# Hybrid delta-rule and attention block: four VectorE/GpSimd assignments and the slot of the v transposes

## The chip, the core and the metric

The kernel runs on one core of a Trainium2 chip. A core has five instruction queues that run side by side and meet through semaphores: TensorE (PE, matrix products and transposes, with its weight loads listed as PEld), VectorE (DVE), ScalarE (ACT), GpSimd (POOL) and SyncE (SP, which here issues nearly all DMAs). Each queue runs its instructions in the order in which they were written into it. The metric is the device time of one execution in microseconds; the time before is 1368.79 us, the median of 3 runs (1368.75 to 1371.78).

## The reference, cut to what matters

One layer of a diffusion backbone works on 512 latent tokens and 256 context tokens of width 2048. Both groups of heads read one input projection.

```
h  = rms_norm(x)*(1+scale)+shift          # adaLN; the same for the context hc
qkv_g, z_g, gates, q_a, k_a, v_a, z_a = split(h @ w_in)      # and hc @ w_in
# group A, 8 heads of 128: conv of 5 taps, silu, then per 64-token chunk
a     = strict_lower((k*beta) k^T * decay);  t_inv = (I + a)^-1
v_new = u - w S;  o = (q e^g) S + intra v_new;  S = S e^{g_last} + (k e^{..})^T v_new
o_gdn = o_forward + flip(o_backward)       # two scans, starting from the context's state
gdn   = rms_norm(o_gdn) * silu(z_g)
# group B, 8 query heads on 2 key heads: rms-normed q, k, rotary positions on latents, softmax
attn  = softmax(q k^T) v * silu(z_a)
y     = concat(gdn, attn) @ w_out;   out = rms_norm(x + gate*y)
```

## The kernel before, in words

Products are made from passes on fp32r operands: each 128x512 piece of a weight is loaded (`wraw`), cast on ScalarE to a high part (`whi`, L129), and the low part is the difference of the two (`wlo`, L130). The helper `split` takes the engine of that subtraction as an argument and uses GpSimd where none is given. Three buffers each hold `wraw`, `whi` and `wlo`. Every output needs three matmuls per 128 rows: high by high, high by low activations, low by high.

The kernel has these stages. Up to about 150 us it normalises the input, forms the modulation and projects the first tiles. From about 150 us to 930 us it runs the 8 heads' delta-rule scans one after the other; this is the stage that the change touches. From about 930 us to 1180 us it runs the attention, with the z projections as filler (their `wlo` is on GpSimd too, through `z_piece`). The last stage is the output projection, whose `wlo` (`wlo_wo`) is on VectorE already.

In the scan stage TensorE's order is written out by hand (`manual_schedule` for PE): a scan of one head is a generator with 12 steps, and each step hands TensorE three groups of work with a pause (a slot) between them, 35 slots in all. In a pause, `pull(n)` takes as many columns of matmuls from `feeding()`: the projections of the k, q and v of later heads, of the attention's k, v, q and of some z, all through `proj_steps` (L152 to L180), which fetches one weight piece per 12 or 24 matmuls. A step of the scan has this chain: two matmuls on the state (`ks`, L852, L854), the right side `r` on VectorE (L866, two halves), a matmul with the inverse (`ts`, L875), its scaling on ScalarE (`vs`, `vn`, L879, L882), the update matmuls (L886) and the new state `st` on VectorE (L892). The old state times its decay (`sd`) is formed on GpSimd meanwhile (L240 through `mul`). The pulls of F1, F2 and F3 columns (3900, 2700, 3200) are what TensorE has to do while it waits for `r`, for `vs` and for `st`.

The order on VectorE, ScalarE, GpSimd and SyncE in this stage is set by a planner that simulates the program: an engine takes the ready instruction of the highest priority. Priority follows program order, and blocks marked `first_of_all()` (the scan's own steps) or `soon()` are moved ahead.

Beside the scan of head h, `gdn_prep(h+1)` prepares the next head in steps at the slots `PREP_AT`. The steps before the v transposes make `ktok`, the sums of squares, the gate differences `gr` (L681: a row of cumulated gates minus a column, then L684 and an exponential), the matrix `AT` in place of `gr`, and the inverse of its 16x16 blocks, a chain of 28 small VectorE operations on `NE` (L738, L740). Then two steps transpose v on TensorE and scale it into `vtok` on ScalarE (L751, L753); the second of them also issues four loads of `DD` on SyncE (L758) and one transpose on VectorE (L763). The last four steps finish the inverse into `UU`, whose last parts VectorE copies (L821). At the end of a scan the two directions are added (L902, L903). Beside the scan of the last head runs `attn_prep()`: it norms k and q and calls `rope_apply` three times (L944, through `mul` at L240), which multiplies by the sine table (`rt2`), multiplies in place by the cosine table, and adds.

Of the kernel before, what the change touches and what calls it, by code (L numbers as in the profile page):

```python
# [11 lines left out]
ALU = mybir.AluOpType  # L12
# [56 lines left out]
def build(tc, a):  # L69
    nc = tc.nc  # L70
    V, S, G, T, SY = nc.vector, nc.scalar, nc.gpsimd, nc.tensor, nc.sync
# [31 lines left out]
    def hpass(k, hi, lo):  # L103

        return (hi, [t[:, k] for t in hh]), (hi, [hl(m, k) for m in range(2)]), (lo, [t[:, k] for t in hh])
# [13 lines left out]
    gsc = {}  # L119
# [6 lines left out]
    def split(raw, nm, lo_eng=None):  # L126
        hi = wp.tile([128, 512], F32R, tag="whi", bufs=3, name=f"whi_{nm}")
        lo = wp.tile([128, 512], F32R, tag="wlo", bufs=3, name=f"wlo_{nm}")
        S.copy(hi, raw)  # L129
        (lo_eng or G).tensor_tensor(out=lo, in0=raw, in1=hi, op=ALU.subtract)  # L130
        return hi, lo

    def wpiece(src, nm, shape, lo_eng=None):
        raw = wp.tile([128, 512], F32, tag="wraw", bufs=3, name=f"wraw_{nm}")
        v = raw
        if shape is not None:
            v = raw.rearrange("p (a b) -> p a b", b=shape)
        SY.dma_start(v, src)
        hi, lo = split(raw, nm, lo_eng)
        if shape is not None:  # L140
            hi = hi.rearrange("p (a b) -> p a b", b=shape)
            lo = lo.rearrange("p (a b) -> p a b", b=shape)
        return hi, lo
# [6 lines left out]
    def proj_tile(col, nm, pl, pc=None):  # L150
        for _ in proj_steps(col, nm, pl, pc):
            pass  # L152

    def proj_steps(col, nm, pl, pc=None):


        for kq in range(4):
            src = w_in[kq * 512:(kq + 1) * 512, col:col + 128].rearrange("(k p) c -> p k c", p=128)
            hi, lo = wpiece(src, f"{nm}_{kq}", 128)
            passes = [(kq * 4 + k4, n, lw, rt) for k4 in range(4)  # L160
                      for n, (lw, rt) in enumerate(hpass(kq * 4 + k4, hi[:, k4], lo[:, k4]))]

            def one(out, m, k, n, lw, rt):
                T.matmul(out, lhsT=lw, rhs=rt[m], start=k == 0 and n == 0, stop=k == KT - 1 and n == 2,  # L164
                         skip_group_check=True)

            if pc is not None and kq == 0:
                for out, m, n_ in ((pl, 0, SEQ), (pc, 1, CTX)):
                    for x in passes:
                        one(out, m, *x)  # L170
                        yield n_
                continue
            for x in passes:
                one(pl, 0, *x)
                if pc is not None:
                    one(pc, 1, *x)
                yield SEQ if pc is None else SEQ + CTX
# [11 lines left out]
    def btile(shape, nm):  # L189
        return PB.tile(shape, F32, tag="b", name=nm)  # L190
# [4 lines left out]
    def take(pl, pc, raw=None, eng=None):  # L195

        raw = next_craw() if raw is None else raw
        copy = S.copy if eng is None else eng.tensor_copy
        if pc is not None:
            copy(raw[:, 2:2 + CTX], pc)  # L200
        copy(raw[:, CTX + 4:CTX + 4 + SEQ], pl)
        return raw
# [33 lines left out]
    def silu(eng, out, x, t):  # L236
        eng.scalar_tensor_tensor(out=out, in0=t, scalar=1.0, in1=x, op0=ALU.add, op1=ALU.mult)

    def mul(eng, out, x, y):
        eng.tensor_tensor(out=out, in0=x, in1=y, op=ALU.mult)  # L240
# [347 lines left out]
    def kq_of(h):  # L588
        if h not in kqs:
            kqs[h] = qkp.tile([128, 8, 128], F32, tag="kq", bufs=3, name=f"kq{h}")  # L590
        return kqs[h]

    def gdn_post_k(h, raw):
        kq = kq_of(h)
        kc = kcs[h] = qkp.tile([128, 2, 2, 64], F32, tag="kc", bufs=2, name=f"kc{h}")
        acc, e, off = conv(8 + h, f"k{h}", raw, True)
        x, y = [t[:, off:off + SEQ].rearrange("p (c t) -> p c t", t=64) for t in (acc, e)]
        silu(V, kq[:, 0:4, 0:64], x[:, 0:4], y[:, 0:4])
        silu(V, kq[:, 4:8, 64:128], x[:, 4:8], y[:, 4:8])
        x, y = [t[:, 0:CTX].rearrange("p (c t) -> p c t", t=64) for t in (acc, e)]  # L600
        silu(V, kc[:, :, 0], x[:, 0:2], y[:, 0:2])
        silu(V, kc[:, :, 1], x[:, 2:4][:, ::-1], y[:, 2:4][:, ::-1])
# [18 lines left out]
    def gdn_prep(h):  # L621


        nm = f"h{h}"
        kq, kc, vv = kqs[h], kcs[h], vvs[h]
        UU, IB = UUs[h % 2], IBs[h % 2]
        col = slice(h * 12, h * 12 + 12)
        gr = gp.tile([128, 12, 64], F32, tag="gr", bufs=1, name=f"gr{nm}")
        for s in range(2):
            src = growd[s:s + 1, col].rearrange("s r t -> s (r t)").to_broadcast([64, 768])  # L630
# [7 lines left out]
        t2 = btile([128, 4, 128], f"t2{nm}")  # L638
# [17 lines left out]
        for p in range(2):  # L656
# [18 lines left out]
                        in0=gsc["beta"][:, col].rearrange("p (v q) -> p v q", v=2),  # L675
                        in1=rk2.unsqueeze(1).to_broadcast([128, 2, 6]), op=ALU.mult)
# [1 line left out]
        mul(V, cc[:, 2], cc[:, 0], gsc["esuf"][:, col])  # L678


        G.tensor_tensor(out=gr, in0=gr, in1=gsc["gcum"][:, col].unsqueeze(2).to_broadcast([128, 12, 64]),  # L681
                        op=ALU.subtract)
        for v in range(2):
            V.tensor_tensor(out=gr[:, v * 6:v * 6 + 6], in0=gr[:, v * 6:v * 6 + 6],  # L684
                            in1=masks[v].unsqueeze(1).to_broadcast([128, 6, 64]), op=ALU.min)
# [36 lines left out]
        for half in range(2):  # L722
            for blk in range(2):
                b, bi = half * 64 + blk * 32, half * 2 + blk
                cb = slice(blk * 32, blk * 32 + 32)
                for v in range(2):
                    src = AT[b:b + 32, v * 6:v * 6 + 6, cb] if v == half else NT[b:b + 32, :, cb]
# [6 lines left out]
        with tc.high_priority(offset=1500):  # L734
            for m in range(14, 0, -1):
                n = 15 - m
                tv = tm[:, :m * n].rearrange("w (j i) -> w j i", i=n)
                V.tensor_tensor(out=tv, in0=NE[:, 0:m, m:m + 1].to_broadcast([96, m, n]),  # L738
                                in1=NE[:, m:m + 1, m + 1:].to_broadcast([96, m, n]), op=ALU.mult)
# [44 lines left out]
        for bi in range(4):  # L784
            half, b = bi // 2, bi * 32
            for v in range(2):
                src = (DD if v == half else DT)[b:b + 32, v * 6:v * 6 + 6]
# [36 lines left out]
    def gdn_scan(h):  # L824

        nm = f"h{h}"
        kq, kc = kqs[h], kcs[h]
# [4 lines left out]
        oq = gp2.tile([128, 2, 4, 128], F32, tag="oq", bufs=1, name=f"oq{nm}")  # L832
        osb = oq[:, 0]
        kss = stile([128, 2, 256], f"ks{nm}", "k")
        steps = [(0, 0), (0, 1), (1, 1), (1, 0)] + [(0, p) for p in range(2, 6)] + [(1, p) for p in range(5, 1, -1)]
        for si, (v, p) in enumerate(steps):
# [8 lines left out]
            if si == 0:  # L845
                r = vtok[:, p]
            else:
                ks = kss[:, si % 2].rearrange("q (d e) -> q d e", d=2)
                r = gp2.tile([128, 128], F32, tag="r", bufs=1, name=f"r{nm}_{si}")
# [9 lines left out]
                with first_of_all():  # L859
# [5 lines left out]
                    for rows, d in halves:  # L865
                        V.scalar_tensor_tensor(out=r[rows], in0=ks[rows, d], scalar=gsc["negeg"][rows, gcol:gcol + 1],  # L866
                                               in1=vtok[rows, p], op0=ALU.mult, op1=ALU.add)
# [31 lines left out]
        ms = gp2.tile([128, 4], F32, tag="ms", bufs=2, name=f"ms{nm}")  # L899
        oc = gp2.tile([128, 8, 64], F32, tag="oc", bufs=1, name=f"oc{nm}")  # L900
        jk = oc[:, 0:2].rearrange("p c t -> p (c t)")
        G.tensor_tensor(out=oq[:, 1], in0=osb, in1=oq[:, 1], op=ALU.add)  # L902
        V.tensor_tensor(out=osb, in0=oq[:, 1], in1=o, op=ALU.add)  # L903
        for p in range(4):
            S.activation(jk, osb[:, p], AF.Square, accum_out=ms[:, p:p + 1])
# [15 lines left out]
    def swapped(x):  # L921

        return x.rearrange("p t (a s r) -> p (t a) s r", a=2, s=2)[:, :, ::-1]
# [17 lines left out]

    def rope_apply(y, tb, t2):

        mul(G, t2.rearrange("p t (a s r) -> p (t a) s r", a=2, s=2), swapped(y),  # L944
            tb[:, 1].rearrange("p t (a s r) -> p (t a) s r", a=2, s=2))
        mul(V, y, y, tb[:, 0])
        V.tensor_tensor(out=y, in0=y, in1=t2, op=ALU.add)
# [76 lines left out]
        split_from(tp.rearrange("p t c -> p (t c)"), *A["qt"])  # L1024

    F1, F2, F3 = 3900, 2700, 3200
    PREP_AT = (0, 2, 4, 6, 8, 10, 12, 27, 29, 31, 33)

    def soon():
        return tc.high_priority(offset=1500)  # L1030
# [4 lines left out]
    with tc.high_priority(offset=4000):  # L1035
        raws = [take(klat, cctx[:, 0]), take(qlat, None), take(vlat, cctx[:, 1], None, V),
                take(klat1, cctx1[:, 0], xraw[0]), take(qlat1, None, xraw[1])]
# [24 lines left out]
    def feed_q(h):  # L1062
        pl = PP.tile([128, SEQ], F32, tag="pl", name=f"ql{h}")
        yield from proj_steps(COL_Q + h * 128, f"q{h}", pl)
        gdn_post_q(h, take(pl, None))
# [54 lines left out]
    def pull(n):  # L1120
        debt[0] += n
        while debt[0] > 0:
            c = next(feed, None)
            if c is None:
                debt[0] = 0
                return
            debt[0] -= c

    def run(gen, *pulls):

        for n in pulls:
            pull(n)
            if next(gen, gen) is gen:
                return
        for _ in gen:
            pull(2000)

    g0, g1 = gates(0, 1), gates(1, NH)
# [7 lines left out]
    with first_of_all():  # L1146
        next(g0, None)
    prep = gdn_prep(0)
    for i, n in enumerate((3000, 5500, 5500, 4000, 14000, 6000)):
        pull(n)  # L1150
        next(prep, None)
        if i == 4:
            gdn_post_k(1, raws[3])
    pull(3000)
    next(g1)
    pull(9000)
    with first_of_all():
        next(g1)
    gdn_post_q(1, raws[4])
    es_x.close()  # L1160
    run(g1, 14000)
    es1.close()
    gp2 = es_g.enter_context(tc.tile_pool(name="gp2", bufs=1, reuse_waits="tile"))
    UUs.append(gp2.tile([128, 12, 128], F32, name="UU1"))
# [3 lines left out]
    for h in range(NH):  # L1168
# [3 lines left out]
        if h + 1 < NH:  # L1172
            prep, prep_at = gdn_prep(h + 1), PREP_AT
        else:
# [4 lines left out]
            prep, prep_at = attn_prep(), range(1, 36, 2)  # L1179
# [334 lines left out]
    for c in range(4):  # L1514
# [3 lines left out]
        if c < 3:  # L1518
            ops = [PO.tile([128, 512], F32, tag="po", name=f"po{c}_{t}") for t in range(4)]
            for k in range(KT):  # L1520
                hi, lo = wpiece(w_out[k * 128:(k + 1) * 128, cs_], f"wo{c}_{k}", None, V)
# [6 lines left out]
        for k in range(KT):  # L1528
            hi = op_.tile([128, 512], F32R, name=f"wlh{k}")
            lo = op_.tile([128, 512], F32R, name=f"wll{k}")  # L1530
# [5 lines left out]
        for t in range(4):  # L1536
# [5 lines left out]
            f = fr[:, t:t + 1]  # L1542
# [36 lines left out]
```

## Time and profile before

| what | us |
|---|---|
| median of 3 runs (lowest, highest) | 1368.79 (1368.75, 1371.78) |
| the profiled execution | 1373.23 |
| its span, first to last instruction | 1371.5 |
| GpSimd busy in the span | 458.2 |
| VectorE busy in the span | 781.6 |
| TensorE busy in the span | 1271.3 |

The profiled execution lies 4.4 us above the median, and 1.7 us of it lie outside the span. Busy time of an engine is the time in which at least one of its instructions ran. In the list of waits a row names the engine, what the waiting instruction makes and its line, what it waited for, and then the sum of the waits in us, their number and the longest. In a timeline a row has the start, the duration, the engine, the line, the operation, output and inputs, and in brackets the idle time of the engine just before and what ended it. PEclk is the clock granted to TensorE as a share of full speed.

### The profile page before, as it was taken

To read this page: it belongs to the slowest core of one execution; us is meant where nothing else is said; L and a number is where in the kernel's file an instruction comes from. 1 tells how busy PE (TensorE), PEld (TensorE's weight loads), DVE (VectorE), ACT (ScalarE), POOL (GpSimd) and SP (SyncE) were. 2 spreads that over 40 slices of the span, in tenths; PEclk is the share of its full clock that TensorE was granted. 3 is DMA by queue.
4 is the path that set the end of the run, shared out by engine and by line. 5 is a ranking of instruction groups with operands and counts; after the bars stand their busy time and mean duration, and the time that the engine had idled before them with its cause. 6 is when DMAs were issued, how large, how long until landed. Compare 5 with 4: busy or idle time off the path is not lost. (4 is left out here: it accounts for less than half of the span.)

```text
span 1371.5 us, 24428 instructions
## 1 busy us (share of the span) xinstructions
PE 1271.3 (93%) x9226; PEld 1032.2 (75%) x9226; DVE 781.6 (57%) x1662; ACT 583.7 (43%) x1464; POOL 458.2 (33%) x437
## 2 busy tenths in 40 slices
PE   6899998999899999999899998998999999999997
PEld 4566777877788778877787777777888788777785
DVE  5455594766846666485664524316788877544322
ACT  4222542535345454544545434434455444433211
POOL 1323232434344253434334344443233232020330
PEclk9999999999999999999999999999999999999998
DMA  9999233221332223231222443347344343564212
GB/s 342 323 334 348 56 94 85 60 63 44 71 75 70 50 66 65 71 72 53 51 59 70 98 128 100 89 135 226 108 124 146 100 130 109 189 225 146 92 39 92
DMA packets 227001, 164.54 MB, mean 120 GB/s; under 512 B 62210, under 2 KB 198491, under 8 KB 225859
## 3 DMA queue, kind: packets, MB, share of 16 engines
q1 hardware_dynamic: 226586, 162.87, 40.9%
q8 instruction: 73, 1.20, 0.4%
q14 instruction: 45, 0.37, 0.1%
q10 hardware_dynamic: 297, 0.11, 0.0%
HBM read 148.85 MB, written 14.08 MB: 119 GB/s over the span
## 5 line engine op out<-in xcount | busy, mean ns | idle before, releaser
L130 POOL TENSOR_TENSOR wlo_z<-wraw_z,whi_z 128x512 fp32r<-128x512 f32 x44 | 67.3, 1544 | 141.0 <-ACT whi_z L129 128.3
L240 POOL TENSOR_TENSOR sdh<-sth,egl 128x256 f32<-128x256 f32 x80 | 55.1, 689 | 144.4 <-DVE sth L892 99.7
L866 DVE SCALAR_TENSOR_TENSOR rh<-ksh,negeg,vtokh 64x128 f32<-64x128 f32 x176 | 61.3, 348 | 55.3 <-PE ksh L854 45.5
L871 ACT ACTIVATE oqh<-ksh,egsw 64x128 f32<-64x128 f32 x128 | 46.4, 362 | 103.7 <-DVE rh L866 95.8
L147 PE MATMUL po<-wlo_wo,mh 128*128 128x512 f32 x192 | 77.7, 405 | 3.7 <-DVE wlo_wo L130 3.7
L892 DVE TENSOR_TENSOR sth<-sdh,tsh 128x256 f32<-128x256 f32 x80 | 33.6, 419 | 80.3 <-PE tsh L886 73.1
L148 PE MATMUL po<-whi_wo,ml 128*128 128x512 f32 x192 | 77.6, 404 | 0.0
L146 PE MATMUL po<-whi_wo,mh 128*128 128x512 f32 x192 | 76.9, 403 | 0.5 <-ACT whi_wo L129 0.5
L130 DVE TENSOR_TENSOR wlo_wo<-wraw_wo,whi_wo 128x512 fp32r<-128x512 f32 x48 | 37.7, 793 | 63.8 <-ACT whi_wo L129 63.8
L1360 PE MATMUL zl<-hhL,whi_z 128*128 128x512 f32 x176 | 74.0, 421 | 0.0
L1360 PE MATMUL zl<-hhL,wlo_z 128*128 128x512 f32 x176 | 69.7, 396 | 0.1
L1360 PE MATMUL zl<-hL,whi_z 128*128 128x512 f32 x176 | 69.6, 396 | 0.0
L886 PE MATMUL tsh<-vsh,ktok 128*128 128x128 f32 x352 | 58.2, 289 | 8.7 <-ACT vsh L879 5.6
L886 PEld LDWEIGHTS tsh<-vsh,ktok 128*128 128x128 f32 x352 | 49.1, 197 | 18.8 <-ACT vsh L879 8.7
L1401 DVE SCALAR_TENSOR_TENSOR gacc<-graw,scol,gacc 128x512 f32<-128x512 f32 x60 | 60.0, 1000 | 1.2
L1510 POOL TENSOR_TENSOR yx<-yx,tt 128x512 f32<-128x512 f32 x12 | 17.2, 1445 | 127.9 <-DVE tt L240 127.9
L130 POOL TENSOR_TENSOR wlo_v<-wraw_v,whi_v 128x512 fp32r<-128x512 f32 x28 | 38.1, 1362 | 59.3 <-ACT whi_v L129 59.2
L129 ACT CAST whi_wo<-wraw_wo 128x512 fp32r<-128x512 f32 x48 | 29.3, 618 | 64.9 <-PE po L148 47.9
L875 PE MATMUL tsh<-rh,UU 128*128 128x128 f32 x176 | 36.9, 292 | 18.7 <-DVE rh L866 18.5
L879 ACT ACTIVATE vsh<-tsh,cch 128x128 f32<-128x128 f32 x88 | 32.3, 367 | 46.0 <-PE tsh L875 44.8
L221 DVE SCALAR_TENSOR_TENSOR cacc_v<-craw,cvT,cacc_v 128x512 f32<-128x512 f32 (+1 forms) x64 | 44.1, 734 | 10.5 <-ACT cacc_v L217 10.2
L875 PEld LDWEIGHTS tsh<-rh,UU 128*128 128x128 f32 x176 | 28.7, 190 | 28.3 <-issue 20.4
(542 smaller groups left out, 4147.8 us busy)
## 6 DMA issues: line engine op xcount, KB each, us to landing
wada<-in_w_ada SPq DMA_DIRECT2D x64, 512.0 KB, 8.6
graw<-in_w_ada SPq DMA_DIRECT2D x64, 256.0 KB, 3.3
wraw_wo<-in_w_out SPq DMA_DIRECT2D x48, 256.0 KB, 2.8
wraw_z<-in_w_in SPq DMA_DIRECT2D x44, 256.0 KB, 3.1
wraw_v<-in_w_in SPq DMA_DIRECT2D x28, 256.0 KB, 2.8
wraw_k<-in_w_in SPq DMA_DIRECT2D x24, 256.0 KB, 2.8
wraw_q<-in_w_in SPq DMA_DIRECT2D x24, 256.0 KB, 2.9
xs<-in_x SPq DMA_DIRECT2D x4, 1024.0 KB, 7.4
```

The costliest lines, as they stand in the source:

```text
L130: (lo_eng or G).tensor_tensor(out=lo, in0=raw, in1=hi, op=ALU.subtract)
L146: T.matmul(out, lhsT=lh, rhs=rh, start=start, stop=False, skip_group_check=True)
L147: T.matmul(out, lhsT=lh, rhs=rl, start=False, stop=False, skip_group_check=True)
L148: T.matmul(out, lhsT=ll, rhs=rh, start=False, stop=stop, skip_group_check=True)
L221: V.scalar_tensor_tensor(out=x, in0=raw[:, i0 + j:i0 + j + m], scalar=w(j), in1=x, op0=ALU.mult, op1=ALU.add)
L240: eng.tensor_tensor(out=out, in0=x, in1=y, op=ALU.mult)
L866: V.scalar_tensor_tensor(out=r[rows], in0=ks[rows, d], scalar=gsc["negeg"][rows, gcol:gcol + 1], in1=vtok[rows, p], op0=ALU.mult, op1=ALU.add)
L871: S.activation(oq[rows, v, p - 2], ks[rows, d], AF.Copy, scale=gsc["egsw"][rows, gcol:gcol + 1])
L875: T.matmul(ts[:, 2], lhsT=UU[:, w], rhs=r, start=True, stop=True, skip_group_check=True)
L886: T.matmul(ts[:, d], lhsT=ktok[:, p, half], rhs=vs, start=True, stop=True, skip_group_check=True)
L1360: T.matmul(pl, lhsT=lw, rhs=rt, start=k == 0 and m == 0, stop=k == KT - 1 and m == 2, skip_group_check=True)
L1401: V.scalar_tensor_tensor(out=acc, in0=raw, scalar=scol[:, k:k + 1], in1=acc, op0=ALU.mult, op1=ALU.add)
```

## The change

It gives the low parts of the weight pieces of `proj_steps` to VectorE, and with them the subtraction of the gate differences (L681), the sum of the two directions' state outputs (L902) and the sine product of `rope_apply`. The two steps of `gdn_prep` that transpose v move from slots 10 and 12 to slots 15 and 18. For head 0, whose preparation runs before the first scan, the first v transpose moves behind the first two steps of the gates of heads 1 to 7 (`g1`), with the same total of pulled columns (64000) around it. The pieces of the z projections in the attention stage, of the first projection and of the output projection stay as they are.

```
@@ proj_steps
-            hi, lo = wpiece(src, f"{nm}_{kq}", 128)
+            hi, lo = wpiece(src, f"{nm}_{kq}", 128, V)
@@ gdn_prep
-        G.tensor_tensor(out=gr, in0=gr, in1=gsc["gcum"][:, col].unsqueeze(2).to_broadcast([128, 12, 64]),
+        V.tensor_tensor(out=gr, in0=gr, in1=gsc["gcum"][:, col].unsqueeze(2).to_broadcast([128, 12, 64]),
                         op=ALU.subtract)
@@ gdn_scan
-        G.tensor_tensor(out=oq[:, 1], in0=osb, in1=oq[:, 1], op=ALU.add)
+        V.tensor_tensor(out=oq[:, 1], in0=osb, in1=oq[:, 1], op=ALU.add)
@@ rope_apply
-        mul(G, t2.rearrange("p t (a s r) -> p (t a) s r", a=2, s=2), swapped(y),
+        mul(V, t2.rearrange("p t (a s r) -> p (t a) s r", a=2, s=2), swapped(y),
             tb[:, 1].rearrange("p t (a s r) -> p (t a) s r", a=2, s=2))
@@ build
-    PREP_AT = (0, 2, 4, 6, 8, 10, 12, 27, 29, 31, 33)
+    PREP_AT = (0, 2, 4, 6, 8, 15, 18, 27, 29, 31, 33)
@@ build, before the first scan
-    for i, n in enumerate((3000, 5500, 5500, 4000, 14000, 6000)):
+    for n in (3000, 5500, 5500, 4000, 14000):
         pull(n)
         next(prep, None)
-        if i == 4:
-            gdn_post_k(1, raws[3])
-    pull(3000)
+    gdn_post_k(1, raws[3])
+    pull(9000)
     next(g1)
     pull(9000)
     with first_of_all():
         next(g1)
     gdn_post_q(1, raws[4])
     es_x.close()
-    run(g1, 14000)
+    pull(7000)
+    next(prep, None)
+    run(g1, 7000)
```

## The prediction

> **What bounds the kernel now.** I read the page's busy times first, then the stretches of the scan stage, then the waits of TensorE, then the timeline around single waits.
>
> ```profile
> PE 1271.3 (93%) x9226; PEld 1032.2 (75%) x9226; DVE 781.6 (57%) x1662; ACT 583.7 (43%) x1464; POOL 458.2 (33%) x437
> ```
>
> TensorE is the bound, and what is to be had is its idle time and its slow time. The change touches 150 to 930 us; in the next rows the first two figures behind the stretch are its length and TensorE's busy time, then PEld, DVE, ACT, POOL, and the granted clock.
>
> ```profile
> 150.00:200.00 50.00, 45.81 (x263) 37.60 (x262) 41.78 (x110) 28.18 (x67) 16.50 (x22) 1.00 0.27 69
> 150.00:250.00 100.00, 91.11 (x788) 76.25 (x786) 67.69 (x175) 45.26 (x111) 32.91 (x37) 0.98 0.31 76
> 250.00:820.00 570.00, 531.24 (x5039) 446.56 (x5037) 342.82 (x860) 270.11 (x763) 228.44 (x225) 0.99 0.28 68
> 820.00:930.00 110.00, 98.70 (x484) 80.24 (x483) 33.41 (x73) 45.36 (x129) 50.10 (x47) 0.95 0.40 113
> ```
>
> Idle: 8.9 + 38.8 + 11.3 = 59.0 us. Slow clock: 2% of 100, 1% of 570 and 5% of 110, 2.0 + 5.7 + 5.5 = 13.2 us. So 72 us at most in these stages. Whom TensorE waits for (sum, times, longest):
>
> ```profile
> PE tsh L875 <- DVE rh L866: 18.5, 14, 3.4
> ...
> PE ksh L852 <- DVE sth L892: 7.0, 10, 1.2
> PE tsh L875 <- DVE UU L821: 6.7, 3, 2.9
> PE tsh L886 <- ACT vsh L879: 5.6, 8, 2.0
> PE tvh L751 <- DVE grh L240: 3.9, 2, 1.9
> ...
> PE qtp L955 <- DVE ktok L947: 2.6, 1, 2.6
> ```
>
> TensorE never waits for a `wlo`. It waits for VectorE: 18.5 + 7.0 + 6.7 + 3.9 + 2.6 = 38.7 us. Yet VectorE is busy only 60% of the middle stretch, so the question is why it is late. Around 367 us:
>
> ```profile
> 366.50 1.99 POOL L130 TENSOR_TENSOR wlo_v<-wraw_v,whi_v 128x512 fp32r<-128x512 f32 x1 [0.16 <-ACT whi_v L129]
> ...
> 367.25 1.27 DVE L740 TENSOR_TENSOR NEh<-NEh,tmh 96x26 f32<-96x26 f32 x1
> 368.56 0.19 DVE L738 TENSOR_TENSOR tmh<-NEh 96x36 f32<-96x36 f32 x1
> ...
> 370.23 0.46 PE L875 MATMUL tsh<-rh,UU 128*128 128x128 f32 x2 [1.26 <-DVE rh L866]
> ```
>
> A VectorE operation on 26 elements takes 1.27 us, and its larger neighbour 0.19: it is held while GpSimd forms a low part, and released as that ends (368.49 and 368.52). `rh` follows 1.1 us late and TensorE idles 1.26. At the start of head 1's scan three GpSimd operations, all of them moved by this change, do this in turn (first fence GpSimd, second VectorE, third TensorE):
>
> ```profile
> 318.73 1.58 POOL L130 TENSOR_TENSOR wlo_k<-wraw_k,whi_k 128x512 fp32r<-128x512 f32 x1 [1.91 <-ACT whi_k L129]
> 320.27 1.45 POOL L902 TENSOR_TENSOR oqh<-oqh 128x512 f32<-128x512 f32 x1
> 321.69 1.65 POOL L681 TENSOR_TENSOR grh<-grh,gcum 128x768 f32<-128x768 f32 x1
> ```
>
> ```profile
> 318.68 0.48 DVE L221 SCALAR_TENSOR_TENSOR cacc_v<-craw,cvT,cacc_v 128x256 f32<-128x256 f32 x1
> 319.08 1.51 DVE L237 SCALAR_TENSOR_TENSOR vv<-craw,cacc_v 128x256 f32<-128x256 f32 x1
> 320.51 1.49 DVE L221 SCALAR_TENSOR_TENSOR cacc_v<-craw,cvT,cacc_v 128x256 f32<-128x256 f32 x1
> ```
>
> ```profile
> 325.98 0.46 PE L875 MATMUL tsh<-vtokh,UU 128*128 128x128 f32 x2 [2.87 <-DVE UU L821]
> ```
>
> So GpSimd's time is partly VectorE's time too. The Trainium skill, SBUF — State Buffer, section "Who interferes with whom", has this as a rule: a VectorE instruction with two SBUF inputs contends with a GpSimd one that reads SBUF, and the loser blocks for all of the other's duration; these rows agree (1.27 against 0.19).
>
> **The change part by part.** Counts and the price of a low part on either engine (the columns of the first four rows: stretch, its length, VectorE and GpSimd time in L130; of the fifth: min/median/max in ns):
>
> ```profile
> 150.00:200.00 50.00, 0.00 (x0) 13.34 (x11) 1.00 0.27 69
> 150.00:250.00 100.00, 0.00 (x0) 25.91 (x20) 0.98 0.31 76
> 250.00:820.00 570.00, 0.00 (x0) 137.00 (x102) 0.99 0.28 68
> 820.00:930.00 110.00, 0.00 (x0) 32.77 (x25) 0.95 0.40 113
> L130 DVE TENSOR_TENSOR wlo_wo<-wraw_wo,whi_wo x48: 671/693/1759, 1168.2 to 1310.3; 128x512 fp32r<-128x512 f32 x48
> ```
>
> The code makes 36 tiles of 4 pieces in `proj_steps`, 144 low parts (the rows show 147, with those that cross a border). GpSimd loses 144 x 1.33 = 192 us. VectorE gains 144 x 0.69 = 99 us, 8 gate differences of 768 (estimated 0.69 x 1.5 = 1.0 each, 8 us), 8 sums and 3 sine products of 0.69 (8 us): 115 us on 444 busy in 780. That is 72% before what the holds give back. Terms:
>
> 1. *v transposes, slots 15 and 18.* The two waits on `grh` (3.9 us) are transposes that want a PSUM bank which the multiplication by `cc` and `gq` still reads; five slots later, more than 11 us by the slot time below, it is long free. −3.9 (0 if the same wait turns up at the new slots). The step also moves ScalarE scalings, the four `DD` loads on SyncE's queue and a VectorE transpose. What needs them is slot 27. A head takes 570/7 = 81 us for 35 slots, 2.3 us each, so nine slots are 21 us of cover. On SyncE the loads move behind weight loads that now come earlier, and TensorE waits for no `wlo` and no `whi` in this stage: 0.
>
> 2. *`rope_apply`.* Three waits of TensorE are behind it: 3.4 us (the longest on `rh`), 2.6 (`qtp`), and 1.98 (the last row).
>
> ```profile
> 868.82 1.27 POOL L240 TENSOR_TENSOR rt2k<-ktok,IB 128x512 f32<-128x512 f32 x1 [0.81 <-PE zal1a L164]
> ...
> 870.05 1.26 POOL L130 TENSOR_TENSOR wlo_z1a<-wraw_z1a,whi_z1a 128x512 fp32r<-128x512 f32 x1
> 870.13 1.73 DVE L240 TENSOR_TENSOR ktok<-ktok,IB 128x512 f32<-128x512 f32 x1 [1.38 <-POOL rt2k L240]
> ...
> 841.68 0.46 PE L875 MATMUL tsh<-rh,UU 128*128 128x128 f32 x2 [1.98 <-DVE rh L866]
> ```
>
> VectorE stood still 1.38 us because the in-place product must not overtake `rt2`, was then held by a low part (1.73 for 0.69), and `rh` came behind it. With all three on VectorE the chain is 0.58 shorter, and the hold of 1.04 goes: 1.7 from this wait, nearly all of the 1.98 (its chain has the same hold), 0.7 of the 2.6. −4.4 (0.69 more for each if `rh` gets ahead; 0 if not).
>
> 3. *UU, heads 1 and 5* (2.87 and, by the list, 2.9). The three holds of 1.58 + 1.45 + 1.65 = 4.7 us become VectorE work of 0.69 + 0.69 + 1.0 = 2.4 if it stays in front: 2.3 each, −4.6; 5.8 if not.
>
> 4. *The other waits on `rh` and `sth`*: 18.5 + 7.0 − 3.4 − 2.0 = 20.1. Each sits behind an operation held by some 1.1 us (1.27 for 0.18). Where the low part falls in the same place it costs 0.69, 0.4 less; where the planner, which now counts it on the right engine, puts it elsewhere, all is gained. Between 37% (7.4) and all, and not all holds are low parts (`sd` stays on GpSimd): half, −10.
>
> 5. *Clock.* After a wait of about 2 us and more TensorE runs at half clock:
>
> ```profile
> 326.60:330.00 3.40, 3.40 (x15) 3.13 (x14) 1.72 (x4) 2.63 (x10) 0.00 (x0) 0.51 0.21 61
> ```
>
> That costs 1.7 us each, 13.2 in all as above. About half of these waits are among terms 1 to 3: −6.6. The Trainium skill, TensorE: Matmul & The Clock Gate, Part 1, lets the clock fall after an idle window of about 3.4 us, so by it only the waits of that length would count and the term would be some −2; here a wait of 2.87 was enough.
>
> 6. *What VectorE's new load costs.* From 150 to 200 us it is busy 41.8 of 50 and gets 11 x 0.69 = 7.6: full. TensorE idles 4.2 us there now, and has no slack behind VectorE. I take +4 (0 to 7.6). In the rest there are 176/2 = 88 steps with two handovers to VectorE, whose load goes from 60% to about 70%; +3, from 0 to rival C.
>
> ```profile
> L866 DVE SCALAR_TENSOR_TENSOR rh<-ksh,negeg,vtokh 64x128 f32<-64x128 f32 x176 | 61.3, 348 | 55.3 <-PE ksh L854 45.5 <-PE ksh L857 8.3
> ```
>
> 7. *Added wait.* Each `wlo` waits on VectorE for its `whi` from ScalarE; queued behind it are `rh`, `st`, the conv; TensorE waits for those. ScalarE already carries the casts between `vs` and `vn` in the same kind of queue, and TensorE's wait for it is small (5.6 us), so within term 6.
>
> Sum: −3.9 − 4.4 − 4.6 − 10 − 6.6 + 7 = −22.5. The profiled 1373.2 would become 1350.7. It lies 4.4 above the median of the runs, so the forecast is 1368.8 − 22.5 = 1346. GpSimd alone gains nothing: it is on no path.
>
> **The rivals.** A, more goes: all of the 38.7 and two thirds of the slow clock (9), less 1: 1368.8 − 47 = 1322. For it: nearly every such wait has a held VectorE operation ahead. Against: 1.1 us per hold is replaced, not removed.
>
> B, it evens out: every low part stays in front of what was held, 0.4 gained per hold, and the extra load eats terms 1 to 4: 1367 (1365 to 1372). The Trainium skill, Perfetto Trace Analysis, section "Optimizing Scalar/DVE Operations", leans this way: these two engines share an SBUF port, so shifting work between them might not help. The rows say that the work shrinks by it, 1.33 to 0.69, which the port sharing would not undo.
>
> C, slower: VectorE takes a `wlo` whose cast is not there, and stands. The output projection shows such waits:
>
> ```profile
> DVE wlo_wo L130 <- ACT whi_wo L129: 63.8, 30, 5.4
> ```
>
> That is 2.1 us each, on a VectorE with nothing else to do. If they fall in front of `rh` or `st` without cover, 11 of the 144 (23 us) undo the 22.5; at 22 it is 46 − 22.5 = +24, 1392. Against: the planner gives a queue what is ready first, and TensorE's pulls cover part.
>
> D, the change doesn't do what it says: the tiny moves at head 0 or a reordered queue cancel terms 1 and 2. Counted in B.
>
> **How the numbers follow.** Forecast 0.70 (1333 to 1361), A 0.10, B 0.11, C 0.09. Within 0.3% (4.1 us, about what a measurement of this kernel can tell) is 1364.7 to 1372.9. Faster 0.80 (forecast and A), same 0.11, slower 0.09. The range 1322 to 1367 leaves out C, half of B and some of A.
>
> **What would show it.** GpSimd busy near 240 us (458 less 192 and 27 for the other moved operations), VectorE near 850 (782 and 115, less some 40 holds of 1.1); no operation of `NE` or `vv` over 1 us beside a low part; no wait of `tvh` on `grh`; the sum of waits on `rh` under 10 us; granted clock above 0.985. Wrong would be: new waits of TensorE for `wlo`, VectorE idle on `whi`, or waits on `rh` as large as before with VectorE unheld.

## The result, and the profile after

The changed kernel takes 1327.8 us (median of 4 runs, 1326.39 to 1330.68) beside 1370.1 us for the kernel before in the same comparison: a ratio of 0.9693 (95% interval 0.967 to 0.9717), so 42 us less. The forecast was 1346; the direction and the mechanism were right, the size came out nearer to rival A. The profiled execution went from 1373.23 to 1326.56 us, its span from 1371.5 to 1324.8.

The page of the changed kernel shows where the work went: GpSimd lost 217 us of busy time, VectorE gained only 51, less than half of the 115 us of work that moved to it by the prediction's count.

```profile
PE 1259.1 (95%) x9226; PEld 1022.9 (77%) x9226; DVE 832.2 (63%) x1825; ACT 583.8 (44%) x1464; POOL 241.2 (18%) x274
```

The scan stage now runs from 150 to about 890 us. Its three stretches, with the same columns as before (length, TensorE, PEld, VectorE, ScalarE, GpSimd, granted clock):

```profile
150.00:250.00 100.00, 94.59 (x813) 79.56 (x811) 71.40 (x207) 48.87 (x123) 4.40 (x7) 0.98 0.31 76
250.00:790.00 540.00, 528.84 (x5050) 444.94 (x5049) 382.74 (x983) 270.48 (x762) 78.67 (x114) 1.00 0.30 73
790.00:900.00 110.00, 104.90 (x530) 85.14 (x529) 50.68 (x98) 52.03 (x141) 17.33 (x20) 0.98 0.51 152
```

TensorE's idle time is 5.4 + 11.2 + 5.1 = 21.7 us where it was 59.0: 37 us. The slow clock costs 2% of 100 and 2% of 110, 4.2 us where it was 13.2: 9 us. Together that is 46 us. The two sets of stretches do not end at the same point of the program, though. Cut at the same matmuls, the stage has these two rows, before and after (869 matmuls lie ahead of the first cut in both; the second cut is the first transpose of the attention, `pt`):

```profile
150.00:939.70 789.70, 730.69 (x6348) 610.49 (x6347) 446.99 (x1112) 364.98 (x1009) 315.24 (x311) 0.98 0.31 78
149.60:891.50 741.90, 720.73 (x6347) 603.77 (x6348) 498.24 (x1274) 364.94 (x1008) 99.40 (x139) 1.00 0.33 83
```

It is 47.8 us shorter: 37.8 us of TensorE's idle time (59.0 to 21.2) and 10.0 us of its busy time, about what six spells of half clock fewer give at 1.7 us each. The rest of the kernel is 1.1 us longer, which gives the 46.7 us by which the two spans differ. The list of TensorE's waits in the changed kernel:

```profile
PE tsh L886 <- ACT vnh L882: 3.0, 5, 1.1
PE tsh L886 <- ACT vsh L879: 3.0, 5, 0.9
PE tsh L875 <- DVE rh L866: 2.9, 6, 0.8
PE qtp L955 <- DVE ktok L947: 2.8, 1, 2.8
...
PE kvl L164 <- DVE wlo_kv L130: 2.1, 1, 2.1
PE kvl L164 <- DVE craw L201: 2.1, 1, 2.1
PE tsh L875 <- DVE UU L821: 2.0, 4, 0.9
...
PE ksh L852 <- DVE sth L892: 0.2, 1, 0.2
```

The wait on `rh` fell from 18.5 to 2.9 us, on `sth` from 7.0 to 0.2, on `UU` from 6.7 to 2.0, and `tvh` is not in the list any more. The holds themselves can be seen in the small operations of the chain on `NE` (L740: min/median/max in ns), first in the kernel before, then in the changed one:

```profile
L740 DVE TENSOR_TENSOR NEh<-NEh,tmh x112: 168/200/1274, 210.5 to 781.3; 96x14 f32<-96x14 f32 x16, 96x26 f32<-96x26 f32 x16, 96x36 f32<-96x36 f32 x16, 96x44 f32<-96x44 f32 x16
```

```profile
L740 DVE TENSOR_TENSOR NEh<-NEh,tmh x112: 169/200/608, 206.6 to 743.3; 96x14 f32<-96x14 f32 x16, 96x26 f32<-96x26 f32 x16, 96x36 f32<-96x36 f32 x16, 96x44 f32<-96x44 f32 x16
```

The median is the same 200 ns; the longest went from 1274 to 608, now that the decay `sd` (618 ns in the median) is what mostly stays on GpSimd there. With the decay on VectorE too (e9 below) the longest is 215:

```profile
L740 DVE TENSOR_TENSOR NEh<-NEh,tmh x112: 163/199/215, 207.1 to 738.4; 96x14 f32<-96x14 f32 x16, 96x26 f32<-96x26 f32 x16, 96x36 f32<-96x36 f32 x16, 96x44 f32<-96x44 f32 x16
```

### The profile page after: what moved, and what is told of

It reads as the page before. It is cut to its first block, busy times and chain, and to the rows that moved or that the text cites. A ratio compares the mean times of both kernels' runs of the same rounds, so it can differ in the third digit from the quotient of the medians.

```text
span 1324.8 us, 24375 instructions
## 1 busy us (share of the span) xinstructions
PE 1259.1 (95%) x9226; PEld 1022.9 (77%) x9226; DVE 832.2 (63%) x1825; ACT 583.8 (44%) x1464; POOL 241.2 (18%) x274
## 5 line engine op out<-in xcount | busy, mean ns | idle before, releaser
L147 PEld LDWEIGHTS po<-wlo_wo,mh 128*128 128x128 f32 x192 | 36.6, 190 | 15.1 <-DVE wlo_wo L130 6.6
L950 ACT CAST pth<-pt 128x512 fp32r<-128x512 f32 x48 | 26.9, 585 | 48.0 <-PE pt L1289 48.0
L164 PE MATMUL vl<-hhL,wlo_v 128*128 128x512 f32 x112 | 46.3, 413 | 0.0
L164 PE MATMUL vl<-hhL,whi_v 128*128 128x512 f32 x112 | 46.2, 413 | 0.0
L146 PEld LDWEIGHTS po<-whi_wo,mh 128*128 128x128 f32 x192 | 36.4, 190 | 12.7 <-ACT whi_wo L129 2.6
```

What stands on the lines that cost most here:

```text
L146: T.matmul(out, lhsT=lh, rhs=rh, start=start, stop=False, skip_group_check=True)
L147: T.matmul(out, lhsT=lh, rhs=rl, start=False, stop=False, skip_group_check=True)
```

## The experiments

The theory under test (H): while GpSimd reads SBUF, VectorE's operations on SBUF operands are held, and in the scan it is that hold which TensorE waits for. Rivals: the gain is the later slots (S); GpSimd's queue was too long, and `sd` and the like came late (Q); the planner's new order on VectorE is better by itself (O). All ratios are to the kernel before, with 95% intervals. A difference in us between two versions is one of medians; the kernel before measured 1370.1 to 1372.1 us in the five comparisons, so about 2 us of such a difference can come from the comparison.

**e1, the low parts alone.**

```
-            hi, lo = wpiece(src, f"{nm}_{kq}", 128)
+            hi, lo = wpiece(src, f"{nm}_{kq}", 128, V)
```

> Only the 144 low parts of the projection pieces go to VectorE; slots, gate differences, sum of outputs and sine products stay as before. Theory H (GpSimd's low parts hold VectorE's operations on SBUF operands, and the hold is what TensorE waits for): most of the gain comes back, 1335 to 1347 us against 1370, the waits of the scan's matmul on rh fall from 18.5 to under 6 us, the two waits of the v transposes (3.9 us) stay. Rival S (the gain is the later slots and the changed order around them): 1360 to 1370, waits on rh near 18.

Measured 1340.25 us, 0.9774 (0.9753 to 0.9794). Of TensorE's waits:

```profile
PE tvh L751 <- DVE grh L240: 5.9, 2, 3.0
...
PE kvl L164 <- DVE wlo_kv L130: 4.7, 1, 4.7
PE tsh L875 <- DVE UU L821: 4.7, 4, 1.5
...
PE tsh L875 <- DVE rh L866: 3.3, 7, 1.0
```

Most of the wait on `rh` (3.3 left of 18.5) goes with the low parts alone; the v transposes wait longer than before (5.9 for 3.9), with a fuller VectorE (829 us busy, 782 before). Three quarters of the gain come from this one line, against S.

**e2, the slots alone.** The changed kernel with all four kinds of operation back on GpSimd.

> Only the v transposes move (slots 15 and 18, and the order before the first scan); all four kinds of operation stay on GpSimd. Theory H: the waits of tvh (3.9 and 3.8 us) go and one or two spells of half clock with them, 1359 to 1366 us; waits on rh stay at 15 to 20 us. Rival S: 1330 to 1345.

Measured 1365.8 us, 0.9957 (0.9941 to 0.9974): 6 us. The wait on `rh` is 16.2 us, and the 3.9 us of `tvh` on `grh` are gone. The 3.8 us of `tvh` on `gts`, which I expected to go as well, are still there (3.5): it is not the new order before the first scan that takes them away.

**e3, gate differences, sum of outputs and sine products alone.**

```
-        G.tensor_tensor(out=gr, in0=gr, ...
+        V.tensor_tensor(out=gr, in0=gr, ...
-        G.tensor_tensor(out=oq[:, 1], ...
+        V.tensor_tensor(out=oq[:, 1], ...
-        mul(G, t2...
+        mul(V, t2...
```

> Only the gate differences, the sum of outputs and the sine products go to VectorE. Theory H: they are 27 us of GpSimd's time against 192 us of the low parts, so a small gain: the two long waits on UU (2.9 us each) and the two long ones on rh during the last scan shrink by about half, with some half clock, 1358 to 1366 us. Rival S: no change, 1366 to 1372.

Measured 1361.66 us, 0.9929 (0.9911 to 0.9947): 10 us. The longest wait on `rh` fell from 3.4 to 1.8 us. The wait on `UU`, which I expected to shrink by half, did not fall (7.2, longest 2.9); the low parts around it are still on GpSimd. Most of the 10 us is clock: in the profiled executions TensorE's idle time is 98.3 us where it was 100.2, and the granted clock is 0.986 where it was 0.979.

**e4, all but the low parts.**

> The changed kernel with the low parts back on GpSimd. Theory H: e2 and e3 together, 1348 to 1362 us, with waits on rh of 10 to 16 us; the low parts are then worth 20 us or more. Rival S: 1328 to 1338.

Measured 1353.51 us, 0.9873 (0.9854 to 0.9891), waits on `rh` 13.6 us. Inside the changed kernel the low parts are thus worth 1353.5 − 1327.8 = 26 us. The three parts by themselves (31 + 6 + 10 = 47 us) give a little more than all at once (42).

**e5 and e6, unused work on GpSimd.** To tell the hold from the queue and from the order, GpSimd gets back work whose result nobody uses, once with reads and once with writes only. The first operation, on two elements, only ties the work to the moment of the low part; the call in `proj_steps` and the scratch tile `junk` are left out here:

```
+    def idle_work(raw, hi):
+        G.tensor_tensor(out=junk[:, 0:2], in0=raw[:, 0:2], in1=hi[:, 0:2], op=ALU.subtract)
+        G.tensor_tensor(out=junk, in0=junk, in1=junk, op=ALU.subtract)        # e5
+        for n in (512, 512, 256):                                             # e6 instead
+            G.memset(junk[:, 0:n], 0.0)
```

> The changed kernel, and for each of the 144 low parts GpSimd also does work that nobody uses: two elements of the high and low part (so that it comes at that time), then a subtraction of a 128x512 scratch tile from itself, which reads SBUF for about 1.3 us. TensorE's order is the same as in the changed kernel, VectorE's up to three rows. Theory H (it is the hold by SBUF reads): the holds come back, 1345 to 1362 us against 1328, operations of the NE chain of over 1 us reappear, waits on rh over 8 us. Rival Q (GpSimd's queue was too long, so that the old state's decay and the like came late): also slower, by as much as in the next run. Rival O (the new order on VectorE is what helps): 1326 to 1333.

> The same, but the unused work is three memsets of the scratch tile (512, 512 and 256 elements, about 1.3 us together), which write SBUF and read nothing. GpSimd is as long busy as in the run before and its queue as full. Theory H: no change, 1326 to 1334 us. Rival Q: as slow as the run with the reads, within 5 us. Rival O: 1326 to 1333 in both.

Measured: e5 1362.34 us, 0.9925 (0.9902 to 0.9948), just above what I gave; e6 1331.86 us, 0.9711 (0.9687 to 0.9735). In the groups of GpSimd the unused work is, in e5 and then in e6:

```profile
L153 POOL TENSOR_TENSOR junk<-junk 128x512 f32<-128x512 f32 x144 | 155.6, 1080 | 11.3
```

```profile
L154 POOL MEMSET junk<- 128x512 f32 (+1 forms) x432 | 196.6, 455 | 23.1
```

So the writes keep GpSimd busy even longer than the reads, and cost 4 us by the medians, which is not clear of noise (their interval meets that of the changed kernel), while the reads cost 34.5 us (32 by the ratios). That is more than the 26 us of e4, but in e5 VectorE has the low parts to do as well. In e6 TensorE's idle time is 65.0 us, 65.7 in the changed kernel; the granted clock of the profiled execution is what differs, 0.983 against 0.988. The price of the reads can be seen on VectorE itself, which runs the same 1825 instructions in all of these versions. Its busy time is 832.2 us in the changed kernel; in e5 and in e6 it is:

```profile
PE 1265.8 (93%) x9226; PEld 1022.3 (75%) x9226; DVE 869.4 (64%) x1825; ACT 584.3 (43%) x1464; POOL 432.6 (32%) x563
PE 1263.5 (95%) x9226; PEld 1026.7 (77%) x9226; DVE 833.5 (63%) x1825; ACT 584.3 (44%) x1464; POOL 471.9 (36%) x851
```

The reads make VectorE 37 us longer, the writes 1.3. The waits of TensorE in e5 and in e6:

```profile
PE tsh L883 <- DVE rh L874: 13.7, 20, 1.8
...
PE tsh L894 <- ACT vsh L887: 7.6, 6, 1.8
...
PE ksh L860 <- DVE sth L900: 6.2, 11, 1.2
```

```profile
PE tsh L884 <- DVE rh L875: 2.9, 5, 1.1
```

In e5 the waits on `rh` and `sth` are back (13.7 and 6.2), though nobody uses the unused work (only the buffers of the weight pieces come free after its first operation, in e5 and e6 alike), TensorE's order is the same, and VectorE's differs in three places at most; in e6 the wait on `rh` is the changed kernel's 2.9. This decides against Q (e6 has the longer queue) and against O (the order is the new one in both). What counts is that GpSimd reads SBUF. (Every reading operation that was tried also writes; a read by itself was not run.)

**e11, one input instead of two.** As e5, with four copies of 128x256 within the scratch tile for the subtraction.

> The changed kernel with unused work on GpSimd again, now four copies of 256 elements per low part within the scratch tile: one input read from SBUF instead of two. Theory H as it stands (any read of SBUF by GpSimd holds a VectorE operation with two SBUF inputs): clearly slower than the changed kernel, 1338 to 1362. Narrower theory (only GpSimd operations with two inputs hold it): 1327 to 1334.

Measured 1352.75 us, 0.9862 (0.9836 to 0.9887): 25 us slower than the changed kernel, with waits on `rh` of 10.5 us and VectorE busy for 858.8 us, 27 more than in the changed kernel. A read with one input holds VectorE too; the narrower theory falls.

**e7, the z pieces too.** The attention stage has 44 more such low parts.

```
-        return wpiece(src, f"z{i}_{kq}", 128)
+        return wpiece(src, f"z{i}_{kq}", 128, V)
```

> The changed kernel, with the 44 low parts of the z projections in the attention stage on VectorE too. Theory H: 44 holds of VectorE there (the row sums gacc take 1.0 us in the mean where they take 0.75 without a hold) turn into 44 x 0.69 = 30 us of work; the waits on qTl (8.1 us) shrink, 1318 to 1325 us. Rival: VectorE is busy 80% there and stands ahead of TensorE with the maximum and the low part of the weights' transposes, so the added work comes through: 1332 to 1345.

Measured 1317.43 us, 0.9609 (0.9587 to 0.9631), 10 us below the changed kernel, a little more than expected. The row sums, in the changed kernel and then in e7:

```profile
L1402 DVE SCALAR_TENSOR_TENSOR gacc<-graw,scol,gacc x60: 734/752/1781, 885.0 to 1114.6; 128x512 f32<-128x512 f32 x60
```

```profile
L1402 DVE SCALAR_TENSOR_TENSOR gacc<-graw,scol,gacc x60: 733/748/753, 887.3 to 1105.4; 128x512 f32<-128x512 f32 x60
```

None of the 60 is held any more (at most 753 ns, from 1781), and the wait on `qTl` fell from 8.1 to 3.1 us.

**e8, first and last stage too; e9, the decay too; e10, all of these.** e8 adds to e7 the low parts of the first projection and the 24 output operations, e9 adds to e7 the decay, e10 has both:

```
-                        mul(G, sd, st, (eg if dt_ == 0 else eg[:, ::-1]).to_broadcast([128, 2, 128]))
+                        mul(V, sd, st, (eg if dt_ == 0 else eg[:, ::-1]).to_broadcast([128, 2, 128]))
```

> The changed kernel with the z pieces' low parts on VectorE (as in e7), and with the low parts of the first projection (32) and the 24 operations of the output's first three column blocks on VectorE as well. Theory H: there are few holds left to remove that TensorE waits for (the waits on the output's low parts are 4 us, those on the first stage's activations 3.5), so 2 to 5 us below e7's 1317, 1312 to 1316. Rival (holds count by GpSimd's time, whoever waits): 78 us of GpSimd's time go, against 67 us in e7 for 10 us: 1303 to 1309.

> As e7, and the scan's old state times its decay (80 operations, 0.71 us each on GpSimd) on VectorE too. Theory H with a limit: 43 short holds go (some 14 us of VectorE's time), but 80 x 0.42 = 34 us of work come into the scan's own chain, right behind the new state and ahead of the next right side, with the scan's priority: between 1314 and 1324, no gain clear of noise. Rival (every read of GpSimd that goes is a gain): 1305 to 1312.

> e8 and e9 together: the z pieces, the first and last stages and the state's decay all on VectorE, so that GpSimd keeps the powers, the UU copies and memsets. Theory H: their gains add, 1310 to 1314. Rival (VectorE is now full enough that the decay in the scan's chain costs what the holds gave): 1315 to 1325.

Measured: e8 1316.35 us, 0.959 (0.9561 to 0.9619); e9 1313.96 us, 0.9571 (0.9544 to 0.9598); e10 1308.64 us, 0.9538 (0.9517 to 0.9559). e8 and e9 by themselves do not stand clear of e7 (their intervals meet its own); e8's time is just above what I gave, and GpSimd's time in those stages was hardly waited for. e10 does stand clear of e7, by 9 us, and lies below what H gave; that VectorE would be too full for the decay is refuted. In it GpSimd is almost idle, and it is the fastest version of this study.

```profile
PE 1251.3 (96%) x9226; PEld 1023.1 (78%) x9226; DVE 860.6 (66%) x2005; ACT 584.7 (45%) x1464; POOL 53.7 (4%) x94
```

## Why the prediction was right, and where it was mis-sized

**The mechanism.** The prediction read a hold from single rows, and e5 beside e6 shows it: unused reads on GpSimd cost 34.5 us, unused writes of more GpSimd time 4, not clear of noise. The rule of the Trainium skill that the prediction cited (SBUF — State Buffer, "Who interferes with whom") names exactly this: reads contend, an operation that only writes does not. The other rule of the Trainium skill that the prediction weighed (Perfetto Trace Analysis, "Optimizing Scalar/DVE Operations", that shifting work between these two engines might not help) was rival B's ground. Here shifting 144 low parts gave 31 us by itself (e1): a low part takes 0.69 us on VectorE and 1.33 on GpSimd, and VectorE's busy time rose by 47.5 us only (829.1 from 781.6), where the low parts are 99 us of work.

**The size.** The time lies outside the band of 1333 to 1361 that had a chance of 0.70, on the side of rival A, which had 0.10. What spoke against A was that "1.1 us per hold is replaced, not removed", and this is the step that failed: the five waits of TensorE on VectorE, 38.7 us together, are 7.9 us now (2.9 + 0.2 + 2.0 + 0 + 2.8), and two thirds of the slow clock of the stage went. That the sum also comes near to A's 47 owes something to waits that neither had counted (below).

**Term 1, v transposes (−3.9).** Right: their wait on `grh` is gone. The slots alone are worth 6 us (e2), where 3.9 and a spell of half clock behind one of the two waits would make 5.6. But in e2 other waits moved too (`rh` −2.3, `sth` −2.5, the one on `vnh` +2.0) and the granted clock stayed at 0.979, so it is not shown that the 6 us are these two waits. The four loads and the transpose that moved with them cost nothing that the list of waits shows.

**Term 2, `rope_apply` (−4.4).** Right in sum, wrong in one part. The longest wait on `rh` is now 0.8 us where two were 3.4 and 2.0, but the wait of `qtp` stayed (2.8 for 2.6), where I had 0.7 less. The timeline of the changed kernel's VectorE shows why:

```profile
843.47 0.69 DVE L940 TENSOR_TENSOR ktok<-qps,ssq 128x512 f32<-128x512 f32 x1 [1.12 <-POOL ssq L234]
844.07 0.68 DVE L130 TENSOR_TENSOR wlo_z2a<-wraw_z2a,whi_z2a 128x512 fp32r<-128x512 f32 x1
844.67 0.71 DVE L866 SCALAR_TENSOR_TENSOR rh<-ksh,negeg,vtokh 64x128 f32<-64x128 f32 x2
845.41 0.69 DVE L240 TENSOR_TENSOR rt2q<-ktok,tabq 128x512 f32<-128x512 f32 x1
846.14 0.69 DVE L240 TENSOR_TENSOR ktok<-ktok,tabq 128x512 f32<-128x512 f32 x1
```

A low part and `rh` now stand between the normed q and its sine product, and take what the shorter product gave.

**Term 3, UU (−4.6).** The wait went from 6.7 to 2.0, −4.7. By e1 (4.7 left) and e3 (7.2) it takes both kinds of operation to move. The unused reads of e5 did not bring it back (1.3).

**Term 4, the other waits on `rh` and `sth` (−10).** This is the term that was mis-sized. I took half of 20.1, supposing that many low parts would stay in front of `rh` and cost 0.69 us there. All that is left of the two waits is 2.9 + 0.2 + 0.2 = 3.3, so the term was −17: nearly every low part came to stand on VectorE where TensorE does not wait for it. e1 shows the same with the low parts alone (3.3 left on `rh`).

**Term 5, clock (−6.6).** It was −9 by the stretches: the waits that vanished took seven of the stage's eight spells of half clock with them, where I had assumed half, and one came anew, behind a wait for a low part (2.1 us, see the next term). The one that remained stands behind the wait of `qtp`:

```profile
848.50:851.90 3.40, 3.40 (x13) 2.91 (x12) 1.71 (x3) 0.98 (x3) 0.00 (x0) 0.50 0.28 69
```

**Terms 6 and 7, VectorE's new load (+7).** Too dear. Between 150 and 200 us VectorE is busy 42.68 of 50, not full, though 10 low parts came in: GpSimd is busy 1.71 us there where it was 16.50, so the holds went too. New on TensorE is one wait of 2.1 us for a low part and 0.6 more on `craw`: 2.7 in all that the list shows. The prediction had named new waits for a `wlo`, and VectorE idle on `whi`, as signs of being wrong. The first is this one wait; the second, the waits on casts that rival C feared, do occur:

```profile
DVE wlo_k L130 <- ACT whi_k L129: 17.1, 16, 2.8
...
DVE wlo_v L130 <- ACT whi_v L129: 8.1, 5, 3.5
...
DVE wlo_q L130 <- ACT whi_q L129: 7.0, 5, 2.3
```

That is 32 us of standing still in these three rows, and 71 us in 60 waits over all pieces of this stage. TensorE's waits on `rh` are still 2.9, so nearly all of them fall where TensorE has other work. That the planner and the pulls bring this about was argued; no run tried another placement.

Sum of the terms as measured: −3.9 − 4.7 (UU) − 17 − 9 − some 5 for `rope_apply` + 2.7 = −37; the span moved by 46.7. I had not counted the waits of `tvh` on `gts` (3.8, now none), of `t1h` on `kq` (1.5, now 0.3), of `ks` on the first state (2.3, now 1.3) and of the update on ScalarE's `vsh` (5.6, now 3.0), 8.6 us together; with them it is −46. The first of these stays while the low parts are on GpSimd (3.5 in e2, 3.3 in e4) and is gone with the low parts alone (e1), where the second is 0.3 too. The hold is not shown to be their cause: in e5, where unused reads take the place of the low parts, neither came back (none on `gts`, 0.3 on `kq`). What removed the other two was not separated.

## What to carry to other kernels

Before sharing elementwise work between VectorE and GpSimd, look for VectorE operations of the same shape with two very different durations: if the long ones end with a GpSimd operation, GpSimd's time is being paid for on VectorE, and an operation that is twice as fast on VectorE costs it less than its own duration when it is moved there, as the holds go with it (here 51 us of busy time for 115 us of work). To test it, give GpSimd unused work once with reads and once with memsets; the difference is the price of the hold. And count the second cost of TensorE's waits: of the nine of 1.95 us and longer in this stage of the kernel before, eight had a spell of 3.4 us at half clock behind them, and no shorter wait had one.

## What was not expected of the hardware

Four copies of 128x256 on GpSimd, 0.40 us each in the median, cost 25 us in all, three quarters of what one subtraction of 1.04 us (median) costs per low part (34.5 us). No single operation of the `NE` chain was then held longer than 587 ns, where it was 1089 with the subtraction:

```profile
L750 DVE TENSOR_TENSOR NEh<-NEh,tmh x112: 168/208/587, 210.3 to 766.6; 96x14 f32<-96x14 f32 x16, 96x26 f32<-96x26 f32 x16, 96x36 f32<-96x36 f32 x16, 96x44 f32<-96x44 f32 x16
```

```profile
L748 DVE TENSOR_TENSOR NEh<-NEh,tmh x112: 168/202/1089, 210.7 to 773.4; 96x14 f32<-96x14 f32 x16, 96x26 f32<-96x26 f32 x16, 96x36 f32<-96x36 f32 x16, 96x44 f32<-96x44 f32 x16
```

So the longest hold shrank with the length of a single GpSimd operation, but their sum shrank by little more than a quarter: VectorE's busy time rose by 27 us, where it rose by 37 with the subtraction. Subtracting a tile from itself on GpSimd took 1.04 us, where two different tiles of the same shape took 1.29; no run here says why.
